# A residual block with a SwiGLU: finer steps beside the plain blocks, rms without a reciprocal, the last three down blocks by halves of the tokens

## Chip, cores and metric

The kernel runs on 1 core of one Trainium2 chip. The metric is the device time of one execution in microseconds (us), as the median of several runs. TensorE (PE in the rows) does the matmuls, VectorE (DVE) and ScalarE (ACT) prepare operands and take results out of PSUM, GpSimd (POOL) does four small products at the end, and SyncE (SP) issues the DMAs. Each engine runs its own queue in order and waits on semaphores of the others.

## What is computed

One layer of a streaming encoder on 512 tokens of width 1024, all float32: two gated token mixers, cross attention to 256 memory tokens, a SwiGLU of width 2816 and a final norm. The change touches only the SwiGLU and the norms around it:

```python
def _rms(t, w):
    tf = t.astype(jnp.float32)
    y = tf * lax.rsqrt(jnp.mean(tf * tf, axis=-1, keepdims=True) + EPS)
    return y.astype(t.dtype) * w

def _swiglu(h, w_gate, w_up, w_down):
    return (jax.nn.silu(h @ w_gate) * (h @ w_up)) @ w_down

def reference(...):
    ...
    x = x + _swiglu(_rms(x, norm_ffn_w[l]), w_ffn_gate[l], w_ffn_up[l], w_ffn_down[l])
    return _rms(x, norm_final_w)
```

## The kernel before

**Arithmetic and layout.** Activations lie transposed: `res[0]` to `res[7]` are the residual stream, 128 features by 512 tokens each. Each float32 operand is split into a high part (ScalarE, a cast) and a low part (VectorE, the difference), and a product is three matmuls: high by high, high by low, low by high. `unit()` loads a weight tile R (`wp`, three buffers), and makes H (ScalarE, L100) and L (VectorE, L101) of it. A load into R waits until the last reader of the tile three before it is done.

**The SwiGLU's plain part.** Hidden blocks 0 to 4 are computed plainly: ten blocks of 24 matmuls of 512 columns, `outs[0]` to `outs[9]`, a gate and an up block in turn, from the unnormalised stream. They go to four PSUM buffers `ps_mm`, so that block 4 writes where block 0 was and needs that `plain_act(0)` has read it. `plain_act(j)` multiplies the gate by the norm's factor `n2.b` (VectorE, L1178), takes the silu (ScalarE), multiplies by the up block (L1180) and splits the product into `act[j]`. The table `beside` (L1192 to 1203) says for each block what VectorE and ScalarE do beside it, and both follow the order in which the code is written (`manual_schedule`):

- `squares` and `norm_2`: the sums of squares of the stream. ScalarE squares into one buffer `sq`, VectorE adds. TensorE sums over the features, VectorE computes rsqrt (`rt_n`) in 9 small operations, TensorE transposes and spreads it (`t<-ident,rt_n`), ScalarE copies it to `n2.b` (`rb_n`, L234).
- `sums(i)` and `splits(i)`: combinations of the stream's token halves (`zx`, 10 VectorE operations for one i) and their split into `z_t1` to `z_t4`, operands of the next part.
- `scale_stream`: `rms` is the reciprocal of `n2.b` (VectorE, L1073), and the stream is multiplied by it (L1075, 8 operations), so that later sums need no other factor. What follows adds to the stream scaled so.
- `weight_side(5)`: loads R of group 5, and sums of its quarters (SA, SB), each split into SH and SL, and DH and DL.

**The groups.** Hidden blocks 5 to 21 are computed by a scheme with seven products in place of eight, `group(j)`: products r11, r21, t2, t1, t3, r22, t4 (L1125), each 12 matmuls of 256 columns. Product t2 writes the PSUM buffer of r11 and so waits for ScalarE's copy of it (`t2k<-mm`, L1140). Between products stand down blocks (`down`), which add the part of the output that is ready to the stream; in the first group the first of them follows t3. Here TensorE follows the code; the order on VectorE and ScalarE is set by a scheduler.

**The last part.** Eight last down blocks, j = 0 to 7, of 15 matmuls each, 512 columns, the last one in two halves of 256 tokens. Behind each, VectorE adds to the stream (L1249), ScalarE squares and multiplies by the final weight (L1252). After a half of block 7 comes `n3`: sums on TensorE (`t<-ones`), rsqrt on VectorE, transposes (`t<-ident,rt_n`) to the one PSUM buffer `ps_t`, the final products `fin` (L1261, L1267 on VectorE, L1265 on GpSimd) that read it, and four output DMAs.

Of the kernel before, what the change touches and what calls it, by code (L numbers as in the profile page):

```python
# [16 lines left out]
ALU = mybir.AluOpType  # L17
# [19 lines left out]
def build(tc, a, out):  # L37
# [46 lines left out]
    def f(ap):  # L84
        return ap.bitcast(F32)
# [97 lines left out]
    class Norm:  # L183
# [850 lines left out]
    def act_tile(n):  # L1034
        return fp.tile([P, 2, S], F32R, tag="a", bufs=9, name=uniq(n))
# [11 lines left out]
    def sums(i):
        tiles = [act_tile("zx") for _ in range(3)]
        x12, x1, x2, x3, x4 = [f(x)[:, e].rearrange("p (k c) -> p k c", k=2) for x in tiles for e in range(2)][:5]
        for e in range(2):  # L1050
            k, q = 2 * i + e, 4 + 2 * i + e
            wa, wb = wf_w[:, k : k + 1], wf_w[:, q : q + 1]

            def stt(o, x, w, y, op):
                nc.vector.scalar_tensor_tensor(out=o[:, e], in0=x, scalar=w, in1=y[:, e], op0=ALU.mult, op1=op)  # L1055

            nc.vector.tensor_scalar_mul(x12[:, e], res[k][:, t1], wa)
            stt(x1, res[k][:, t0], wa, x12, ALU.subtract)
            stt(x2, res[q][:, t1], wb, x1, ALU.add)
            stt(x3, res[q][:, t1], wb, x12, ALU.subtract)  # L1060
            stt(x4, res[q][:, t0], wb, x2, ALU.subtract)
        token_sums[i] = x1, x2, x3, x4

    def splits(i):
        x1, x2, x3, x4 = token_sums[i]
        for o, x, sign in (("t2", x2, -1.0), ("t1", x1, -1.0), ("t3", x3, None), ("t4", x4, -1.0)):
            split(zt[o][:, 2 * i : 2 * i + 2, 0], zt[o][:, 2 * i : 2 * i + 2, 1], x, sign)
# [23 lines left out]
    def weight_side(j):  # L1091

        q0, q1 = slice(0, 512), slice(512, 1024)
        w = a["w_fgu"][j - NPLAIN]
        r0 = wp.tile([P, 1024], F32, tag="R", bufs=3, name=uniq("R"))
        r1 = wp.tile([P, 1024], F32, tag="R", bufs=3, name=uniq("R"))
        sa = fw.tile([P, 2, 512], F32, tag="S", bufs=2, name=uniq("SA"))
        sb = fw.tile([P, 2, 512], F32, tag="S", bufs=2, name=uniq("SB"))  # L1100
# [92 lines left out]
    first_weights = []  # L1193
    beside = {
        0: [lambda: squares(range(4))],
        1: [lambda: squares(range(4, 8)), norm_2],
        2: [lambda: sums(0), lambda: plain_act(0)],
        3: [lambda: splits(0)],
        4: [lambda: plain_act(1), lambda: sums(1)],
        5: [lambda: splits(1)],  # L1200
        6: [lambda: plain_act(2), lambda: scale_stream(range(2))],
        7: [lambda: scale_stream(range(2, KC))],
        8: [lambda: plain_act(3), lambda: first_weights.append(weight_side(NPLAIN))],
        9: [],
    }
    plain = [a[n][j] for j in range(NPLAIN) for n in ("w_fg", "w_fu")]
    us = [unit(x) for x in plain[:2]]
    outs = []
    with tc.manual_schedule(engines={mybir.EngineType.DVE, mybir.EngineType.Activation}):
# [31 lines left out]
    for j in range(KC):
        units = down_units(len(PARTS) - 1, j)

        W = S if j < KC - 1 else S // 2
        for c0 in range(0, S, W):
            cs = slice(c0, c0 + W)
            pb = ps_mm()
            down_block(pb[:, :W], len(PARTS) - 1, units, cs)
            nc.vector.tensor_tensor(out=res[j][:, cs], in0=res[j][:, cs], in1=pb[:, :W], op=ALU.add)  # L1249
            n3.add(res[j][:, cs], cols=cs, last=j == KC - 1)  # L1250
            if j < KC - 1:
                nc.scalar.activation(res[j], res[j], AF.Copy, scale=wo_w[:, j : j + 1])  # L1252
                continue
            n3.finish(cols=cs, eps=eps)
            for i in (7, 6, 0, 1, 2, 3, 4, 5):
                if i % 2 == (1 if i > 5 else 0):
                    fin = xwp.tile([P, S], F32R, tag="xw", bufs=16, name=uniq("fin"))
                    f3 = f(fin).rearrange("p (e c) -> p e c", e=2)
                o = f3[:, i % 2]
                if i == j:  # L1260
                    nc.vector.scalar_tensor_tensor(  # L1261
                        out=o, in0=res[i][:, cs], scalar=wo_w[:, i : i + 1], in1=n3.ps, op0=ALU.mult, op1=ALU.mult
                    )
                elif i in (3, 5):
                    nc.gpsimd.tensor_tensor(out=o, in0=res[i][:, cs], in1=n3.b, op=ALU.mult)  # L1265
                else:
                    nc.vector.tensor_tensor(out=o, in0=res[i][:, cs], in1=n3.ps, op=ALU.mult)  # L1267
                if i % 2 == (0 if i > 5 else 1):
                    nc.sync.dma_start(out[i // 2][:, :, cs], f3)
# [80 lines left out]
```

## Time and profile before

| | |
|---|---|
| median of 3 runs | 926.15 us (925.33 to 926.57) |
| the profiled execution | 926.71 us |
| its span | 924.9 us |
| TensorE busy | 892.9 us, 97% |
| VectorE busy | 674.4 us, 73% |
| ScalarE busy | 476.6 us, 52% |

The span runs from the first to the last instruction on record; the execution is 1.8 us longer. The share of TensorE is so high that only two kinds of place are of interest: those at which it waits, and those at which its matmuls are longer than elsewhere. A list of what each engine waited for, a timeline of each engine, and the granted clock in short windows show both.

### The profile page before, as it was taken

Reading aid. Unit: us, or ns where it says so; the run is one execution under the profiler, and the core shown is the slowest. Engines: PE = TensorE matmul, PEld = TensorE weight load, DVE = VectorE, ACT = ScalarE, POOL = GpSimd, SP = SyncE. Lnnn points to the kernel's source line nnn. Section 1 sums busy time; section 2 is a strip of 40 time slices with the busy share of each in tenths; the row PEclk is TensorE's granted clock in tenths of the full one; section 3 lists DMA queues with packets and bytes.
Section 4 is the critical chain, followed back from the end, with each engine's and each line's share of the span. In section 5 each row is a group of like instructions: output and inputs, shape, how many; then the busy total and the mean of one; then the engine's idle time right before and its main releaser. Section 6 shows DMA issues by size and latency. Waiting matters only on the chain.

```text
span 924.9 us, 12952 instructions
## 1 busy us (share of the span) xinstructions
PE 892.9 (97%) x4879; PEld 761.5 (82%) x4879; DVE 674.4 (73%) x1338; ACT 476.6 (52%) x869; POOL 7.1 (1%) x31
## 2 busy tenths in 40 slices
PE   8999999999999999999999998979999999999994
PEld 6898888887888787778888786869999989899983
DVE  6777888787344959957767986887777786788654
ACT  7576674657334748463435854343444444444451
POOL 1000000000000000000000000000000000000001
PEclk9999999999999999999999998989999999999996
DMA  7332222222332131425332131233232332332312
GB/s 243 95 114 69 69 69 69 69 69 69 97 109 69 48 102 58 135 69 172 101 130 99 47 98 62 82 99 110 86 103 93 103 112 93 103 120 68 91 44 91
DMA packets 31726, 86.20 MB, mean 93 GB/s; under 512 B 4304, under 2 KB 8016, under 8 KB 31664
## 3 DMA queue, kind: packets, MB, share of 16 engines
q1 hardware_dynamic: 31520, 85.37, 29.4%
q8 instruction: 38, 0.62, 0.3%
q14 instruction: 24, 0.20, 0.1%
q10 hardware_dynamic: 144, 0.00, 0.0%
HBM read 83.27 MB, written 2.10 MB: 92 GB/s over the span
## 4 chain that ended last, share of the span: by engine, by line
PE 70%; DVE 15%; DMA 7%; ACT 5%; issue 2%; SPq 0%; DVEq 0%; ACTq 0%
PE mm L82 52%; PE mm L1125 7%; DMA R<-in_w_fd 4%; PE s L1125 3%; PE s L82 3%; PE o L82 3%; DVE L L101 2%; DMA R<-in_w_fgu 2%; DVE SL L101 2%; ACT H L100 1%; PE t L82 1%; PE t L551 1%; DVE zx L1055 1%; DMA R<-in_w_tg 1%; ACT pm L96 1%
## 5 line engine op out<-in xcount | busy, mean ns | idle before, releaser
L100 ACT CAST H<-R 128x1024 fp32r<-128x1024 f32 (+4 forms) x137 | 123.8, 905 | 175.8 <-PE mm L82 120.4
L101 DVE TENSOR_TENSOR L<-R,H 128x1024 fp32r<-128x1024 f32 (+4 forms) x137 | 142.5, 1042 | 53.1 <-ACT H L100 52.5
L82 PE MATMUL mm<-xh,H 128*128 128x512 f32 x320 | 125.7, 394 | 3.9 <-DVE t2k L1178 3.9
L82 PE MATMUL mm<-xl,H 128*128 128x512 f32 x320 | 127.4, 398 | 0.0
L82 PE MATMUL mm<-xh,L 128*128 128x512 f32 x320 | 127.2, 398 | 0.0
L82 PE MATMUL mm<-a,H 128*128 128x512 f32 (+1 forms) x362 | 110.2, 386 | 0.0
L82 PEld LDWEIGHTS mm<-a,H 128*128 128x128 f32 x362 | 65.3, 188 | 11.4
L82 PEld LDWEIGHTS mm<-xh,H 128*128 128x128 f32 x320 | 60.9, 190 | 16.6 <-issue 4.3
L82 PE MATMUL mm<-H,xh 128*128 128x512 f32 (+1 forms) x192 | 70.5, 367 | 0.0
L82 PEld LDWEIGHTS mm<-xl,H 128*128 128x128 f32 x320 | 60.8, 190 | 11.7
L82 PE MATMUL mm<-L,xh 128*128 128x512 f32 (+1 forms) x192 | 70.3, 366 | 0.0
L82 PE MATMUL mm<-H,xl 128*128 128x512 f32 (+1 forms) x192 | 70.1, 365 | 0.0
L82 PEld LDWEIGHTS mm<-xh,L 128*128 128x128 f32 x320 | 60.8, 190 | 11.1
L82 PE MATMUL mm<-a,L 128*128 128x512 f32 (+1 forms) x181 | 69.3, 383 | 0.0
L1125 PE MATMUL mm<-z_t,SH 128*128 128x256 f32 x272 | 50.2, 284 | 3.1 <-ACT t2k L1140 2.7
L96 ACT ACTIVATE p<-sm,nm,sc 128x256 f32<-128x256 f32 (+1 forms) x64 | 36.3, 569 | 25.3 <-DVE es L525 20.3
L1125 PEld LDWEIGHTS mm<-z_t,SH 128*128 128x128 f32 x272 | 42.7, 191 | 5.0 <-ACT t2k L1140 3.3
L82 PEld LDWEIGHTS mm<-L,xh 128*128 128x128 f32 x192 | 36.1, 188 | 5.4 <-DVE L L101 0.6
L82 PEld LDWEIGHTS mm<-H,xh 128*128 128x128 f32 x192 | 36.3, 189 | 5.2 <-ACT H L100 0.2
L1125 PE MATMUL mm<-xh,SH 128*128 128x256 f32 x136 | 38.6, 284 | 1.9 <-ACT SH L100 1.9
L82 PEld LDWEIGHTS mm<-H,xl 128*128 128x128 f32 x192 | 36.1, 188 | 5.1
L82 PEld LDWEIGHTS mm<-a,L 128*128 128x128 f32 x181 | 34.0, 188 | 7.0
(354 smaller groups left out, 2095.8 us busy)
## 6 DMA issues: line engine op xcount, KB each, us to landing
R<-in_w_fgu SPq DMA_DIRECT2D x34, 512.0 KB, 4.0
R<-in_w_gate SPq DMA_DIRECT2D x16, 512.0 KB, 3.5
R<-in_w_fd SPq DMA_DIRECT2D x24, 256.0 KB, 2.6
R<-in_w_fd SPq DMA_DIRECT2D x16, 320.0 KB, 2.9
x<-in_xT SPq DMA_DIRECT2D x16, 256.0 KB, 3.3
R<-in_w_q SPq DMA_DIRECT2D x8, 512.0 KB, 3.9
R<-in_w_attn_o SPq DMA_DIRECT2D x8, 512.0 KB, 3.5
R<-in_w_vg SPq DMA_DIRECT2D x8, 512.0 KB, 3.5
```

The source lines that it names most:

```text
L82: nc.tensor.matmul(o, lhsT=lhsT, rhs=rhs, start=start, stop=stop)
L96: last_table[0] = nc.scalar.activation(*args, **kw)
L100: nc.scalar.copy(out=hi, in_=src)
L101: nc.vector.tensor_tensor(out=lo, in0=src, in1=f(hi), op=ALU.subtract)
L551: nc.tensor.transpose(out=pt[:, i * P : (i + 1) * P], in_=prs[i // 2][:, i % 2, b * P : (b + 1) * P], identity=ident)
L1055: nc.vector.scalar_tensor_tensor(out=o[:, e], in0=x, scalar=w, in1=y[:, e], op0=ALU.mult, op1=op)
L1125: nc.tensor.matmul(o, lhsT=l_, rhs=r_, start=first and k == 0 and i == 0, stop=k == 3 and i == 2, skip_group_check=not first,)
```

## The change

It has four pieces.

1. **Steps beside the plain blocks.** `squares` use a tile each pair, not one `sq`. `sums(i)` is called in halves, and its first operation (x12, a multiplication by a weight) goes from VectorE to ScalarE. `norm_2` moves from block 1 to block 2, and `plain_act` becomes a generator whose three steps are placed one by one.
2. **rms.** In place of the reciprocal, `v * rsqrt(v)` is formed on 128x4 values (one VectorE operation), transposed and spread by four more matmuls into the PSUM buffer `o`, and copied by ScalarE to `rms`.
3. **weight_side(5)** is a generator too, started in block 7, and the first down block's weights are loaded in block 9's place (`first_units`) and not when the down block is reached.
4. **The last part.** Blocks 5, 6 and 7 are all done by halves: first tokens 0 to 255 of the three, then tokens 256 to 511.

```diff
-            sq = acc
-            if not first:
+            if first:
+                sq = acc
+            elif sq is None:
                 sq = tp.tile([P, S], F32, tag="sq", bufs=1, name=uniq("sq"))[:, :w]
...
-            nc.vector.tensor_scalar_mul(x12[:, e], res[k][:, t1], wa)
+        nc.scalar.activation(x12[:, e], res[k][:, t1], AF.Copy, scale=wa)
...
-        if js[0] == 0:
-            nc.vector.reciprocal(rms, n2.b)
...
     def norm_2():
         n2.finish()
+        rt = alr[:, 0, NT : 2 * NT]
         nc.vector.tensor_scalar_mul(eps, n2.v, EPS)
+        nc.vector.tensor_tensor(out=rt, in0=n2.v, in1=n2.tok, op=ALU.mult)
+        pb = ps_o()
+        for t in range(NT):
+            mm(pb[:, t * P : (t + 1) * P], rt[:, t : t + 1].broadcast_to([P, P]), ident, True, True)
+        return pb
...
-        2: [lambda: sums(0), lambda: plain_act(0)],
...
+        [lambda: pb.append(norm_2()), lambda: sums(0, 1), lambda: next(acts[0]), lambda: splits(0, ("t2", "t1"))],
...
+        [lambda: scale_stream((4, 5, 6, 7)), lambda: first_units.append(down_units(0, 0))],
...
+    steps = [(j, slice(0, S)) for j in range(KC - 3)]
+    for cs in (t0, t1):
+        steps += [(j, cs) for j in range(KC - 3, KC)]
+    for j, cs in steps:
```

**VectorE behind the second norm.** `rt_n` is the rsqrt, `zx` are the sums of the first pair of features, L1178 (after: L1184) is the first operation of `plain_act(0)`, which block 4 needs. Before:

```order
L181 SCALAR_TENSOR_TENSOR rt_n_1057_5532<-nwt_5534,nwy_5533 128x4
L1189 TENSOR_SCALAR alr<-v_n_1056_5530 128x4
L101 TENSOR_TENSOR L_5553<-R_5551,H_5552 128x1024
L1057 TENSOR_SCALAR zx_5582<-x_0_4470,wf_w 128x256
L1055 SCALAR_TENSOR_TENSOR zx_5582<-x_0_4470,wf_w,zx_5582 128x256
L1055 SCALAR_TENSOR_TENSOR zx_5583<-x_4_4632,wf_w,zx_5582 128x256 x2
L1055 SCALAR_TENSOR_TENSOR zx_5584<-x_4_4632,wf_w,zx_5583 128x256
L1057 TENSOR_SCALAR zx_5582<-x_1_4509,wf_w 128x256
L1055 SCALAR_TENSOR_TENSOR zx_5582<-x_1_4509,wf_w,zx_5582 128x256
L1055 SCALAR_TENSOR_TENSOR zx_5583<-x_5_4673,wf_w,zx_5582 128x256 x2
L1055 SCALAR_TENSOR_TENSOR zx_5584<-x_5_4673,wf_w,zx_5583 128x256
L1178 TENSOR_TENSOR t2k_5595<-mm_5447,rb_n_1061_5548 128x512
```

After:

```order
L181 SCALAR_TENSOR_TENSOR rt_n_1061_5568<-nwt_5570,nwy_5569 128x4
L1204 TENSOR_SCALAR alr<-v_n_1060_5566 128x4
L1205 TENSOR_TENSOR alr<-v_n_1060_5566,rt_n_1061_5568 128x4
L1058 SCALAR_TENSOR_TENSOR zx_5522<-x_1_4509,wf_w,zx_5522 128x256
L1058 SCALAR_TENSOR_TENSOR zx_5523<-x_5_4673,wf_w,zx_5522 128x256 x2
L1058 SCALAR_TENSOR_TENSOR zx_5524<-x_5_4673,wf_w,zx_5523 128x256
L1184 TENSOR_TENSOR t2k_5598<-mm_5447,rb_n_1065_5584 128x512
```

The weight tile's L and the sums' first half now stand ahead of the norm, and both x12 are on ScalarE, so that four operations of `zx` lie between the norm and the first step of `plain_act(0)` and not ten and an L.

**ScalarE at the first group.** H and R are the weights of the down blocks (640 columns) and R of 1024 columns that of group 6; SH and DH belong to the weight sides; the last row is the copy for which product t2 waits. Before:

```order
L100 CAST SH_5847<-R_5841 128x1024
L100 CAST H_6028<-R_6027 128x640
L100 CAST SH_5855<-SB_5844 128x1024
L100 CAST SH_5859<-SA_5843 128x1024
L100 CAST DH_5863<-R_5842 128x512
L100 CAST SH_6056<-R_6050 128x1024
L1140 COPY t2k_5904<-mm_5902 128x256
```

After:

```order
L100 CAST SH_5850<-SB_5811 128x1024
L1189 CAST a_5855<-t2k_5845 128x512
L100 CAST SH_5857<-SA_5810 128x1024
L100 CAST DH_5861<-R_5809 128x512
L100 CAST H_5896<-R_5895 128x640
L100 CAST H_6031<-R_6030 128x640
L100 CAST SH_6059<-R_6053 128x1024
L1143 COPY t2k_5913<-mm_5911 128x256
```

The weight side of group 5 is done earlier against the plain blocks, and the casts of the two down weights stand behind it; the copy stands behind group 6's first cast in both. On SP the load of that R (R_6053) stands behind all loads up to the second down weight, and it goes to the buffer whose last reader is the DL of group 5.

**VectorE at the end.** `fin` are the final products of the first half of the tokens; L1249 (after: L1279) adds a down block to the stream; `acc_n` gathers squares; L223 (after: L224) begins the second half's norm. Before:

```order
L1261 SCALAR_TENSOR_TENSOR fin_8953<-x_7_4755,wo_w,t_8948 128x256
L1267 TENSOR_TENSOR fin_8953<-x_6_4714,t_8948 128x256
L1267 TENSOR_TENSOR fin_8957<-x_0_4470,t_8948 128x256
L1267 TENSOR_TENSOR fin_8957<-x_1_4509,t_8948 128x256
L1267 TENSOR_TENSOR fin_8961<-x_2_4550,t_8948 128x256
L1267 TENSOR_TENSOR fin_8965<-x_4_4632,t_8948 128x256
L223 SCALAR_TENSOR_TENSOR v_n_1591_8993<-t_8988,alr 128x2
```

After:

```order
L1291 SCALAR_TENSOR_TENSOR fin_8956<-x_7_4755,wo_w,t_8951 128x256
L1297 TENSOR_TENSOR fin_8956<-x_6_4714,t_8951 128x256
L1297 TENSOR_TENSOR fin_8960<-x_0_4470,t_8951 128x256
L1297 TENSOR_TENSOR fin_8960<-x_1_4509,t_8951 128x256
L1297 TENSOR_TENSOR fin_8964<-x_2_4550,t_8951 128x256
L1297 TENSOR_TENSOR fin_8968<-x_4_4632,t_8951 128x256
L1279 TENSOR_TENSOR x_6_4714<-x_6_4714,mm_8993 128x256
L1279 TENSOR_TENSOR x_7_4755<-x_7_4755,mm_9014 128x256
L209 TENSOR_TENSOR acc_n_8720<-acc_n_8720,sq_9010 128x256
L224 SCALAR_TENSOR_TENSOR v_n_1593_9038<-t_9033,alr 128x2
```

The first half's final products now stand ahead of the last two additions, and on TensorE the transposes that they need stand 19 matmuls of 256 columns ahead of the last one, where before they stood behind it.

## Rows read from the trace of the kernel before

**Rows 1.** Page, busy time, share of the span and instructions of each engine.

```profile
PE 892.9 (97%) x4879; PEld 761.5 (82%) x4879; DVE 674.4 (73%) x1338; ACT 476.6 (52%) x869; POOL 7.1 (1%) x31
```

**Rows 2.** TensorE's waits from 550 us on: total us, times, longest us.

```profile
PE mm L82 <- DVE t2k L1178: 3.9, 1, 3.9
...
PE t L82 <- DVE fin L1267: 2.7, 1, 2.7
PE mm L1125 <- ACT t2k L1140: 2.7, 1, 2.7
```

**Rows 3.** Window: its length, busy time by engine, PEclk, DMA share, GB/s.

```profile
570.00:575.00 5.00, 5.00 (x12) 3.94 (x13) 3.64 (x5) 4.25 (x8) 0.00 (x0) 0.50 0.03 8
```

**Rows 4.** TensorE at blocks 3 and 4: start, duration, line, operation, operands.

```profile
565.39 0.39 PE L82 MATMUL mm<-xl,H 128*128 128x512 f32 x1
565.62 0.39 PE L82 MATMUL mm<-xh,L 128*128 128x512 f32 x1
...
575.13 0.40 PE L82 MATMUL mm<-xh,H 128*128 128x512 f32 x1
```

**Rows 5.** TensorE, the last plain matmul, product t2, and down block 0.

```profile
604.86 0.39 PE L82 MATMUL mm<-xh,L 128*128 128x512 f32 x1
...
615.52 0.51 PE L1125 MATMUL mm<-z_t,SH 128*128 128x256 f32 x2 [2.68 <-ACT t2k L1140]
...
621.80 0.63 PE L82 MATMUL mm<-a,H 128*128 128x512 f32 x2
```

**Rows 6.** ScalarE: the copy of norm 2, group 6's cast, product t2's copy.

```profile
562.14 0.59 ACT L234 COPY rb_n<-t 128x512 f32<-128x512 f32 x1 [4.99 <-PE t L82]
...
614.15 1.04 ACT L100 CAST SH<-R 128x1024 fp32r<-128x1024 f32 x1
615.11 0.37 ACT L1140 COPY t2k<-mm 128x256 f32<-128x256 f32 x1
```

**Rows 7.** VectorE from norm 2 to the end of group 5's weight side.

```profile
560.67 0.16 DVE L181 SCALAR_TENSOR_TENSOR rt_n<-nwt,nwy 128x4 f32<-128x4 f32 x1
...
563.71 1.23 DVE L101 TENSOR_TENSOR L<-R,H 128x1024 fp32r<-128x1024 f32 x1 [2.80 <-ACT H L100]
564.85 0.35 DVE L1057 TENSOR_SCALAR zx<-x,wf_w 128x256 f32<-128x256 f32 x1
565.24 1.80 DVE L1055 SCALAR_TENSOR_TENSOR zx<-x,wf_w,zx 128x256 f32<-128x256 f32 x4
...
570.42 0.69 DVE L1180 TENSOR_TENSOR t2k<-t2k,mm 128x512 f32<-128x512 f32 x1 [0.70 <-ACT t2k L96]
...
593.02 3.35 DVE L1073 RECIPROCAL rms<-rb_n 128x512 f32<-128x512 f32 x1
...
598.75 3.69 DVE L1075 TENSOR_TENSOR x<-x,rms 128x512 f32<-128x512 f32 x6
...
609.52 0.82 DVE L101 TENSOR_TENSOR L<-R,H 128x640 fp32r<-128x640 f32 x1
...
615.06 0.69 DVE L101 TENSOR_TENSOR DL<-R,DH 128x512 fp32r<-128x512 f32 x1
```

**Rows 8.** Window from the end of `rt_n` to the end of DL, VectorE's busy time alone.

```profile
560.83:615.75 54.92, 44.24 (x68) 0.91 0.25 79
```

**Rows 9.** DMA issues from 590 to 625 us: count, KB each, median us to landing.

```profile
R<-in_w_fgu SPq DMA_DIRECT2D x4, 512.0 KB, 3.8
```

**Rows 10.** TensorE in the last down block, and the norms of its two halves.

```profile
903.00 0.40 PE L82 MATMUL mm<-a,H 128*128 128x256 f32 x2
...
904.79 0.40 PE L82 MATMUL mm<-a,H 128*128 128x256 f32 x2
...
909.32 0.88 PE L82 MATMUL t<-ident,rt_n 128*128 128x128 f32 x4 [1.46 <-DVE rt_n L181]
912.93 0.56 PE L82 MATMUL t<-ones,acc_n 128*128 128x2 f32 x2 [2.72 <-DVE fin L1267]
...
916.69 1.19 PE L82 MATMUL t<-ident,rt_n 128*128 128x128 f32 x4 [1.92 <-DVE rt_n L181]
```

More of the change, by code (lines that the diff above doesn't have):

```diff
@@ L1045, in build, with sums, stt, splits @@
     token_sums = {}
[L1047 to L1055, printed above, removed]
-            nc.vector.tensor_scalar_mul(x12[:, e], res[k][:, t1], wa)
[L1058 to L1065, printed above, removed]
+    def sums(i, e):
+        if e == 0:
+            tiles = [act_tile("zx") for _ in range(3)]
+            xs = [f(x)[:, h].rearrange("p (k c) -> p k c", k=2) for x in tiles for h in range(2)]
+            token_sums[i] = xs[:5]
+        x12, x1, x2, x3, x4 = token_sums[i]
+        k, q = 2 * i + e, 4 + 2 * i + e
+        wa, wb = wf_w[:, k : k + 1], wf_w[:, q : q + 1]
+        def stt(o, x, w, y, op):
+            nc.vector.scalar_tensor_tensor(out=o[:, e], in0=x, scalar=w, in1=y[:, e], op0=ALU.mult, op1=op)
+        nc.scalar.activation(x12[:, e], res[k][:, t1], AF.Copy, scale=wa)
+        stt(x1, res[k][:, t0], wa, x12, ALU.subtract)
+        stt(x2, res[q][:, t1], wb, x1, ALU.add)
+        stt(x3, res[q][:, t1], wb, x12, ALU.subtract)
+        stt(x4, res[q][:, t0], wb, x2, ALU.subtract)
+    def splits(i, which):
+        _, x1, x2, x3, x4 = token_sums[i]
         for o, x, sign in (("t2", x2, -1.0), ("t1", x1, -1.0), ("t3", x3, None), ("t4", x4, -1.0)):
-            split(zt[o][:, 2 * i : 2 * i + 2, 0], zt[o][:, 2 * i : 2 * i + 2, 1], x, sign)
+            if o in which:
+                split(zt[o][:, 2 * i : 2 * i + 2, 0], zt[o][:, 2 * i : 2 * i + 2, 1], x, sign)
     rms = cp.tile([P, S], F32, tag="rb", bufs=2, name="rms")
     def scale_stream(js):
-        if js[0] == 0:
-            nc.vector.reciprocal(rms, n2.b)
         for i in js:
@@ L1179, in plain_act @@
         table_act(t, t, AF.Silu)
+        yield
         nc.vector.tensor_tensor(out=t, in0=t, in1=outs[2 * j + 1], op=ALU.mult)
-        hidden(j, t)
+        act[j] = act_tile("a")
+        nc.scalar.copy(out=act[j][:, 0], in_=t)
+        yield
+        nc.vector.tensor_tensor(out=act[j][:, 1], in0=t, in1=f(act[j][:, 0]), op=ALU.subtract)
+        yield
     def squares(js):
         for i in js:
-            n2.add(res[i])
+            if i % 2 == 1:
+                sqs.append(f(act_tile("sq")))
+            n2.add(res[i], sq=sqs[-1][:, i % 2] if sqs else None)
     def norm_2():
         n2.finish()
+        rt = alr[:, 0, NT : 2 * NT]
         nc.vector.tensor_scalar_mul(eps, n2.v, EPS)
-    eps = alr[:, 0, 0:NT]
[L1193 to L1196, printed above, removed]
-        2: [lambda: sums(0), lambda: plain_act(0)],
[L1198 to L1205, printed above, removed]
+        nc.vector.tensor_tensor(out=rt, in0=n2.v, in1=n2.tok, op=ALU.mult)
[3 more added lines that the diff above has]
+        return pb
+    sqs, first_weights = [], []
+    eps = alr[:, 0, 0:NT]
     plain = [a[n][j] for j in range(NPLAIN) for n in ("w_fg", "w_fu")]
@@ L1208, in build @@
     outs = []
+    pb = []
+    acts = [plain_act(j) for j in range(NPLAIN)]
+    ws = weight_side(NPLAIN)
+    beside = [
+        [lambda: squares(range(4))],
+        [lambda: squares(range(4, 8)), lambda: sums(0, 0)],
+        [lambda: pb.append(norm_2()), lambda: sums(0, 1), lambda: next(acts[0]), lambda: splits(0, ("t2", "t1"))],
+        [lambda: next(acts[0]), lambda: splits(0, ("t3", "t4")), lambda: next(acts[0])],
+        [lambda: next(acts[1]), lambda: sums(1, 0), lambda: next(acts[1]), lambda: sums(1, 1), lambda: next(acts[1])],
+        [lambda: nc.scalar.copy(out=rms, in_=pb[0]), lambda: splits(1, ("t2", "t1", "t3", "t4"))],
+        [lambda: next(acts[2]), lambda: scale_stream((0, 1)), lambda: next(acts[2]), lambda: scale_stream((2, 3)),
+         lambda: next(acts[2])],
+        [lambda: next(ws)],
+        [lambda: next(acts[3]), lambda: next(ws), lambda: next(acts[3]), lambda: first_weights.append(next(ws)),
+         lambda: next(acts[3])],
+        [lambda: scale_stream((4, 5, 6, 7)), lambda: first_units.append(down_units(0, 0))],
+    ]
     with tc.manual_schedule(engines={mybir.EngineType.DVE, mybir.EngineType.Activation}):
@@ L1216, in build @@
                 do()
-        plain_act(NPLAIN - 1)
+        for _ in acts[NPLAIN - 1]:
+            pass
     with tc.manual_schedule(engines={mybir.EngineType.PE}):
@@ L1240, in build @@
     n3 = Norm("n3", S)
[L1241 to L1269, printed above, removed]
@@ new lines, in build @@
+    last = len(PARTS) - 1
+    halved = {}
+    steps = [(j, slice(0, S)) for j in range(KC - 3)]
+    for cs in (t0, t1):
+        steps += [(j, cs) for j in range(KC - 3, KC)]
+    for j, cs in steps:
+        W = cs.stop - cs.start
+        if j not in halved:
+            halved[j] = down_units(last, j)
+        pb = ps_mm()
+        down_block(pb[:, :W], last, halved[j], cs)
+        nc.vector.tensor_tensor(out=res[j][:, cs], in0=res[j][:, cs], in1=pb[:, :W], op=ALU.add)
+        n3.add(res[j][:, cs], cols=cs, last=j == KC - 1)
+        if j < KC - 1:
+            nc.scalar.activation(res[j][:, cs], res[j][:, cs], AF.Copy, scale=wo_w[:, j : j + 1])
+            continue
+        n3.finish(cols=cs, eps=eps)
+        for i in (7, 6, 0, 1, 2, 3, 4, 5):
+            if i % 2 == (1 if i > 5 else 0):
+                fin = xwp.tile([P, S], F32R, tag="xw", bufs=16, name=uniq("fin"))
+                f3 = f(fin).rearrange("p (e c) -> p e c", e=2)
+            o = f3[:, i % 2]
+            if i == j:
+                nc.vector.scalar_tensor_tensor(
+                    out=o, in0=res[i][:, cs], scalar=wo_w[:, i : i + 1], in1=n3.ps, op0=ALU.mult, op1=ALU.mult
+                )
+            elif i in (3, 5):
+                nc.gpsimd.tensor_tensor(out=o, in0=res[i][:, cs], in1=n3.b, op=ALU.mult)
+            else:
+                nc.vector.tensor_tensor(out=o, in0=res[i][:, cs], in1=n3.ps, op=ALU.mult)
+            if i % 2 == (0 if i > 5 else 1):
+                nc.sync.dma_start(out[i // 2][:, :, cs], f3)
```

11 lines of the change are left out of this document (7 added, 4 removed).

## The prediction, as it was put on record

> **What bounds the kernel now.** I read the page's busy times first: TensorE is busy 892.9 of 924.9 us [rows 1]. So nothing that VectorE or ScalarE save counts by itself; it counts where TensorE waits for them. Second, the list of TensorE's waits: the three largest behind the plain blocks' start are at block 4 (3.9 us, for the first step of `plain_act(0)`), at the final norm's second half (2.7 us, for the first half's final products) and at product t2 of the first group (2.7 us, for ScalarE's copy) [rows 2]. Third, the granted clock. After the wait at block 4 it is at 0.50, the 1.2 GHz level, and only 12 matmuls pass in 5 us [rows 3]. So each long wait has a second price behind it. Both together are read as distances between starts:
>
> - Block 4: the last matmul before the wait starts at 565.62, one takes 0.23, and the twelve slow ones end where the next starts, at 575.13 [rows 4]. Thirteen steps of 0.23 would be 2.95 us, they took 9.51: 6.56 us are lost.
> - First group: from the end of the plain part (604.86 + 0.23 = 605.09) to the first down block (621.80) pass 16.7 us [rows 5], for five products of 12 matmuls of 256 columns. At 0.119 each (1.79 us for 15, [rows 10]) that is 7.2: 9.5 us are lost.
> - End: the last down block's matmuls end at 909.32 − 1.46 = 907.86, and the second norm's transposes start at 916.69 [rows 10]. What follows (final products, output DMAs) is the same after the change.
>
> Between the first group and the last part the order of all engines is the same before and after, and the list of waits names none there that comes near these three, so a gain made up to 621.80 is carried to the last part whole.
>
> **The change, part by part.** *Plain part.* The norm's sums stand one matmul later (0.23) and four transposes are added. Four such took 0.88 at the end [rows 10]; I take 0.95, between 0.5 (if they slip in behind others) and 1.2. Is the wait at block 4 gone? `rt_n` ends at 560.83 [rows 7], after the change at 561.06. From there to the copy's end pass 562.14 + 0.59 − 560.83 = 1.9 us [rows 6], then x12 on ScalarE (not shown; between 0.37 for a copy of 256 columns and 0.59 for one of 512, [rows 6]; I take 0.42), four operations of `zx` in 1.80 and the step itself, 0.69 [rows 7]: 565.9. Block 4 can start at 565.85 + 0.23 + 0.95 = 567.0. So the wait goes, by 1.1 us. Plain end: 605.09 − 6.56 + 0.95 = 599.5 (the norm's sums are moved, not added).
>
> *First group.* r11 and r21 find their weights ready, since the weight side now starts in block 7: 24 × 0.113 to 0.119, until about 602.3. Then TensorE needs the copy, and the order on ScalarE puts it behind group 6's cast, which needs group 6's R, whose load waits for DL. In the rows of before, too, the copy came straight after that cast (614.15, then 615.11) [rows 6], while TensorE was in its wait of 2.68 us [rows 5].
>
> So the time of DL decides, not the end of the plain part. From the end of `rt_n` to the end of DL, VectorE was busy 44.24 of 54.92 us, idle 10.7 [rows 8]. Of the busy time go, by [rows 7]: the reciprocal 3.35; four of the six multiplications by rms (4 × 0.615 = 2.46) and two L of 640 columns (2 × 0.82), which now stand behind DL; four x12 (1.40); four `zx` (1.80) and one L (1.23), now ahead of the norm; one split of an act (0.69), now behind DL. The 128x4 product adds 0.16. 44.24 − 12.57 + 0.16 = 31.8. The idle time I take as 9.4: eight places where the order makes VectorE wait for one or two ScalarE operations, at 0.7 (as at L1180, [rows 7]) to 1.7 each. Three of the eight are the x12, each of which VectorE now takes from ScalarE. Bounds: 5.6 (all eight at 0.70) and 10.7 (as before). DL then ends at 561.06 + 31.8 + 9.4 = 602.3 (598.5 to 603.6), and before at 615.75.
>
> From there: load 3.8 [rows 9], cast 0.96 to the next start, copy 0.41 to the start of t2 (615.52 − 615.11) [rows 5, 6]: t2 starts at 607.5. TensorE will have waited 5.2 us, longer than the 2.68 before, so I take the stretch behind it as it was, slow matmuls included: 621.80 − 615.52 = 6.28 [rows 5]. Down block 0 starts at 613.8 in place of 621.80: **8.0 us gained** (6.7 to 11.8). The 6.56 of block 4 is no separate term: it moves the wait to t2, where VectorE's chain ends.
>
> A rule speaks against the x12 move. On VectorE one took 0.35 [rows 7]; on ScalarE it costs VectorE a wait where it isn't covered, 0.70 at L1180 [rows 7]. The Trainium skill, "ScalarE: Activation LUTs", "Rules for kernel authors", gives multiplications to VectorE and not to ScalarE. By the rule the move lengthens the chain by three times 0.35; if instead the x12 were wholly covered, three waits of 0.70 would fall out of the idle time, DL would come 2.1 sooner, and the gain here would be 10.1. I go with the bare wait; no row of before shows this operation on ScalarE.
>
> *rms.* The reciprocal is in the sum above. ScalarE's copy of `rms` (0.59) lies beside blocks; if ScalarE were late there, the multiplications would wait, and with them DL, one for one; that is within the bounds of the idle time.
>
> *Last part.* Two more blocks by halves: a pair of halves is 2 × 1.79 = 3.58 against 15 × 0.227 = 3.40 [rows 4, 10], so +0.4 us. The first half's sums and transposes now stand between matmuls: 0.88 for the transposes more ahead of the last matmul, and some 0.3 for a wait on `rt_n`. Last matmul: 907.86 + 1.6 = 909.4. The first half's transposes start some 3.2 us ahead of that, at 906.2, and copy and final products took 912.93 − 909.32 = 3.6 from there [rows 10], so VectorE has them behind it at 909.8. Then follow one another an addition, and on ScalarE a square, a multiplication and a square, 0.37 to 0.42 each by the copy of 256 columns [rows 6]: 911.5. The second norm's sums are complete from there, and don't begin at 912.93 behind the final products [rows 10]: 1.4 us sooner. One of its four pairs of sums doesn't need the last square (0.4 to 0.56 sooner, [rows 10]), and at the full clock all are shorter. I take **2.1 us** (0 to 2.8).
>
> Sum: 8.0 + 2.1 = 10.1. The profiled execution took 926.71, so 916.6; it lies 0.56 above the median of the runs shown, so a median of 916.0 to 916.6. I say 916.3.
>
> **The rivals.**
>
> *No wait at t2.* If VectorE idles under 4 us up to DL, t2 starts at once: down block 0 at 599.5 + 7.2 = 606.7, 15.1 gained, with the end 17.2: 909.5. For it: no reciprocal, fewer handoffs in a row. Against: eight known waits at 0.70 are already 5.6.
>
> *The wait at block 4 stays.* The margin is 1.1 us. Then the plain part ends at about 606, r21 at 609, and the copy of 607.5 is there: no wait at t2, down block 0 at some 613.5. It costs almost nothing: 916 to 917.
>
> *The end gives nothing,* if the first half's final products keep VectorE until the second half is late by as much as it now is: 926.7 − 8.0 = 918.7. For it: they now stand ahead of the last two additions on VectorE. Against: only 1.7 us of other work follows them up to the sums.
>
> *Slower: the handoffs.* From `rt_n` to DL I count 29 VectorE operations that read a ScalarE result. The new order alternates the two engines more finely. If each handoff cost 0.70 us bare, none covered, VectorE would idle 20.3 us and DL end at 613.2: t2 at 618.4, down block 0 at 624.7, 2.9 later than before, and the end's 2.1 doesn't pay for it: 927.5. It decides at 0.67 us per handoff (19.5 us idle); at 1 us it would be 936. Against it: about as many in the old order left 10.7 us idle in all [rows 8].
>
> *In between,* VectorE idle 13 to 19 us: 920 to 926.
>
> **How the numbers follow.** Forecast 0.62; block 4 still waits 0.07; the end gives nothing 0.12; no wait at t2 0.05; in between 0.08; slower 0.06. The range reaches from 912 (idle time at its lower bound, with the end's best) to 921 (the end gives nothing and the idle time is 1 us over its upper bound); it leaves out no wait, slower and most of in between, 0.17. About 0.2%, 1.85 us, is what a measurement here can tell from no change. Faster by more than that: 0.91 (all but slower and a part of in between); within it 0.04; slower 0.05.
>
> **What would show it.** In the profile after: TensorE without a wait at block 4 and no clock of 0.50 there; L1184 ending about a microsecond ahead of block 4; a wait of 4 to 7 us at t2 for the copy L1143, that copy right behind group 6's cast, that cast behind a load issued when DL ends near 602; a slow stretch behind it; down block 0 near 614; at the end the sums of the second half near 903 to 904, that is some 2 us sooner after the shift of 8 is taken off. If DL comes before 598 or after 606, or the copy comes ahead of the cast, the sum is wrong there; if L1151's waits in the groups grow, the gain was not carried.

## The result, and the profile after

| | before | after |
|---|---|---|
| median | 925.74 us (924.15 to 926.57) | 914.59 us (912.96 to 915.40) |
| ratio | | 0.9879, 95% interval 0.9859 to 0.9899 |
| profiled execution | 926.71 us | 915.01 us |
| its span | 924.9 us | 913.2 us |

The change makes the kernel 11.2 us faster; the forecast was 916.3, some 10 us. The busy times, on the page of the kernel after (busy time, share, instructions of each engine):

```profile
PE 888.4 (97%) x4917; PEld 760.6 (83%) x4917; DVE 670.3 (73%) x1338; ACT 479.3 (52%) x878; POOL 7.0 (1%) x31
```

Against [rows 1], VectorE has lost 4.1 us, ScalarE has gained 2.7, and TensorE is busy 4.5 us less although it has 38 matmuls more; part of that is the low clock behind block 4, which is gone (windows below). TensorE's waits from 545 us on, the four largest of the kernel after (total, times, longest):

```profile
PE mm L1128 <- ACT t2k L1143: 6.0, 2, 5.7
PE t L82 <- DVE rt_n L181: 1.9, 1, 1.9
PE s L1128 <- DVE s L1154: 1.7, 4, 0.7
PE t L82 <- DVE acc_n L209: 1.7, 1, 1.7
```

Of [rows 2] the wait of block 4 and that for `fin` are gone, and the one for ScalarE's copy at t2 has grown from 2.7 to 5.7 us. The three places of the prediction, one after another:

TensorE behind block 4 and behind the wait at t2, in windows of the kernel after (length, busy by engine, granted clock, DMA share, GB/s):

```profile
570.00:575.00 5.00, 5.00 (x24) 4.14 (x23) 3.63 (x5) 2.78 (x5) 0.00 (x0) 1.00 0.37 112
...
605.00:610.00 5.00, 2.63 (x12) 2.63 (x13) 4.81 (x8) 2.46 (x4) 0.00 (x0) 0.50 0.53 179
610.00:615.00 5.00, 5.00 (x33) 4.74 (x33) 4.06 (x7) 2.38 (x4) 0.00 (x0) 0.85 0.27 76
```

The window that passed 12 matmuls at 0.50 [rows 3] now passes 24 at 1.00. Behind t2 a slow stretch remains: the clock is at 0.50 from 605 to 610.

TensorE's rows of the kernel after, at the end of the plain part, product t2 and down block 0 (start, duration, operation, and in brackets the idle time ahead and who ended it):

```profile
598.45 0.39 PE L82 MATMUL mm<-xh,L 128*128 128x512 f32 x1
...
607.37 0.80 PE L1128 MATMUL mm<-z_t,SH 128*128 128x256 f32 x2 [5.71 <-ACT t2k L1143]
...
613.52 0.63 PE L82 MATMUL mm<-a,H 128*128 128x512 f32 x2
```

What t2 waits for, link by link: VectorE's DL, SyncE's issue of group 6's load, ScalarE's cast of it and the copy behind (kernel after):

```profile
601.51 0.68 DVE L101 TENSOR_TENSOR DL<-R,DH 128x512 fp32r<-128x512 f32 x1
```

```profile
602.22 0.33 SPq L1102 DMA_DIRECT2D R<-in_w_fgu  x1
```

```profile
606.00 1.04 ACT L100 CAST SH<-R 128x1024 fp32r<-128x1024 f32 x1 [3.90 <-DMA R<-in_w_fgu]
606.96 0.37 ACT L1143 COPY t2k<-mm 128x256 f32<-128x256 f32 x1
```

Each row begins where the one above ends: DL ends at 602.19, the load is issued at 602.22, ScalarE is idle 3.90 us until it has landed, casts, copies, and t2 starts. In the kernel before, DL did not hold t2: group 6's load was issued 5.4 us ahead of DL's end, and t2 started 0.2 us ahead of it (615.52 against 615.75 [rows 5, 7]).

```profile
610.37 0.33 SPq L1101 DMA_DIRECT2D R<-in_w_fgu  x1
```

So DL ends 13.6 us sooner after the change, and t2 starts only 8.15 us sooner: the 5.2 us of load, cast and copy now come behind DL.

The end, TensorE in the kernel after: the first half's transposes and the matmul behind them, the last down matmul, the second half's sums and transposes:

```profile
896.65 0.68 PE L82 MATMUL t<-ident,rt_n 128*128 128x128 f32 x4
897.09 0.36 PE L82 MATMUL mm<-a,L 128*128 128x256 f32 x1
...
899.32 0.28 PE L82 MATMUL mm<-a,L 128*128 128x256 f32 x1
901.29 0.35 PE L82 MATMUL t<-ones,acc_n 128*128 128x2 f32 x2 [1.70 <-DVE acc_n L209]
901.65 0.59 PE L82 MATMUL t<-ones,sq 128*128 128x2 f32 x2
...
905.01 1.19 PE L82 MATMUL t<-ident,rt_n 128*128 128x128 f32 x4 [1.92 <-DVE rt_n L181]
```

The first half's transposes stand between matmuls, and the second half's sums come 1.7 us behind the last matmul; before they came 5.1 behind it [rows 10].

Between these places, the last addition to the stream in the groups (VectorE), before and then after:

```profile
879.40 0.69 DVE L1174 TENSOR_TENSOR x<-x,mm 128x512 f32<-128x512 f32 x1
```

```profile
870.30 0.69 DVE L1179 TENSOR_TENSOR x<-x,mm 128x512 f32<-128x512 f32 x1
```

So the 11.7 us of the two spans divide as follows: 621.80 − 613.52 = 8.3 up to down block 0; (879.40 − 621.80) − (870.30 − 613.52) = 0.8 in the groups; (924.9 − 879.40) − (913.2 − 870.30) = 2.6 in the last part.

### The profile page after: what moved, and what is told of

The parts are those of the page before. It is cut to its first block, busy times and chain, and to the rows that moved or that the text cites. A ratio compares the mean times of both kernels' runs of the same rounds, so it can differ in the third digit from the quotient of the medians.

```text
span 913.2 us, 13045 instructions
## 1 busy us (share of the span) xinstructions
PE 888.4 (97%) x4917; PEld 760.6 (83%) x4917; DVE 670.3 (73%) x1338; ACT 479.3 (52%) x878; POOL 7.0 (1%) x31
## 4 chain that ended last, share of the span: by engine, by line
PE 78%; DVE 11%; DMA 4%; ACT 4%; issue 2%; SPq 0%; DVEq 0%; ACTq 0%
PE mm L82 55%; PE mm L1128 10%; PE s L1128 4%; PE s L82 3%; PE o L82 3%; DMA R<-in_w_fd 2%; DVE L L101 2%; DMA R<-in_w_fgu 1%; DVE SL L101 1%; PE t L82 1%; DMA x<-in_xT 1%; ACT H L100 1%; PE t L552 1%; ACT SH L100 1%; ACT pm L96 1%
## 5 line engine op out<-in xcount | busy, mean ns | idle before, releaser
L82 PEld LDWEIGHTS mm<-a,H 128*128 128x128 f32 x382 | 67.6, 189 | 10.6
L82 PE MATMUL mm<-a,L 128*128 128x512 f32 (+1 forms) x191 | 71.2, 373 | 0.0
L82 PEld LDWEIGHTS mm<-a,L 128*128 128x128 f32 x191 | 36.0, 188 | 6.5
L101 DVE TENSOR_TENSOR SL<-SB,SH 128x1024 fp32r<-128x1024 f32 x17 | 20.8, 1226 | 24.8 <-ACT SH L100 24.8
```

What stands on the lines that cost most here:

```text
L82: nc.tensor.matmul(o, lhsT=lhsT, rhs=rhs, start=start, stop=stop)
L101: nc.vector.tensor_tensor(out=lo, in0=src, in1=f(hi), op=ALU.subtract)
```

## Experiments

**Theory:** two independent gains. The larger one is set by VectorE's chain from the second norm to DL, by way of group 6's load, cast and copy; the wait at block 4 costs nothing of its own as long as t2 waits longer. The smaller one is the last part. **Rivals:** the gain at the front is the wait at block 4 itself; it comes from the finer steps and not from the reciprocal; the last part's gain is only a shift. All ratios are to the kernel before on the same chip. `c0_after` is the kernel after once more. e1, e3 and e4 ran beside it, e2, e5, e6 and e7 later on the same chip, e9 and e10 on another.

> The changed kernel once more, beside the experiments on the same chip: 914 to 915 us, 11 below the kernel before. In its profile the wait at product t2 for the copy L1143 is 5.5 to 6 us, block 4 doesn't wait, and the first down block starts near 613.5.

Measured: 915.27 us, ratio 0.9874 (0.9855 to 0.9893), t2 at 606.66 behind a wait of 5.69 us, last addition in the groups at 870.81.

**The last part taken back** (`e1_tail_whole`), and **the last part alone, on the kernel before** (`e2_tail_halves`: the same loop the other way round):

```diff
-    steps = [(j, slice(0, S)) for j in range(KC - 3)]
-    for cs in (t0, t1):
-        steps += [(j, cs) for j in range(KC - 3, KC)]
-    for j, cs in steps:
...
+    for j in range(KC):
...
+        W = S if j < KC - 1 else S // 2
+        for c0 in range(0, S, W):
```

> The changed kernel, but the last part as before (down blocks 0 to 6 whole, block 7 in halves). If the last part gave its own gain (the second half's sums no longer behind the first half's final products), 2.1 us (as predicted) to 2.6 us (as the two traces differ there) are lost: 917. Rival, that the shift seen there is only the groups' and the plain part's gain carried on: no change, 914.6. All up to the last part is as in the changed kernel.

> The kernel before with the new last part alone (down blocks 5 to 7 by halves). The change with the old last part lost 3.1 us, so if the last part's gain stands by itself it is 2.5 to 3.1 us here too: 923 to 924 against 926 to 927 of before. Rival, that it needs what comes ahead: no change.

Measured: e1 918.39, 0.9913 (0.9898 to 0.9927), 3.1 us over c0. e2 923.33, 0.9962 (0.9950 to 0.9975), 3.2 under the kernel before. TensorE's row of the second half's sums in e1, and then in e2:

```profile
904.05 0.56 PE L82 MATMUL t<-ones,acc_n 128*128 128x2 f32 x2 [2.72 <-DVE fin L1293]
```

```profile
910.75 0.35 PE L82 MATMUL t<-ones,acc_n 128*128 128x2 f32 x2 [1.70 <-DVE acc_n L208]
```

The wait for `fin` comes and goes with the loop, whatever happens ahead. The piece is worth 3.1 to 3.2 us and adds to the rest; that it gives nothing is excluded. What is left of the change, e1 against the kernel before, is 926.84 − 918.39 = 8.4 us.

**The reciprocal put back** (`e3_reciprocal`), in the place where ScalarE's copy of `rms` now stands:

```diff
-        [lambda: nc.scalar.copy(out=rms, in_=pb[0]), lambda: splits(1, ("t2", "t1", "t3", "t4"))],
+        [lambda: nc.vector.reciprocal(rms, n2.b), lambda: splits(1, ("t2", "t1", "t3", "t4"))],
```

> The changed kernel, but rms is again the reciprocal on VectorE (3.35 us), in the place where the copy from PSUM stood, without the four transposes and the 128x4 product. If VectorE's chain from the norm to DL sets the start of product t2, DL and with it the whole rest come 3.2 us later, the wait at t2 grows to about 9 us (the plain part ends 0.95 sooner) and the time is 917.8. Rival, that TensorE's plain part sets it and the wait at t2 has slack: 0.95 faster, 913.6.

Measured: 920.14, 0.9927 (0.9915 to 0.9940), 4.9 over c0 and 2.3 over what was expected. VectorE and TensorE in e3:

```profile
582.73 3.35 DVE L1220 RECIPROCAL rms<-rb_n 128x512 f32<-128x512 f32 x1
...
604.89 0.68 DVE L101 TENSOR_TENSOR DL<-R,DH 128x512 fp32r<-128x512 f32 x1
```

```profile
590.31 0.47 PE L82 MATMUL mm<-xh,H 128*128 128x512 f32 x1 [2.12 <-DVE t2k L1184]
...
610.81 0.79 PE L1128 MATMUL mm<-z_t,SH 128*128 128x256 f32 x2 [6.55 <-ACT t2k L1143]
```

From the end of `rt_n` to the end of DL pass 45.0 us (560.55 to 605.57) where c0 has 41.8 (559.68 to 601.51): 3.2 longer for 3.35 us of work, nearly one for one. The remaining 0.9 by which DL and t2 are late against c0 lies ahead of `rt_n`, where the two kernels are the same. The new wait of 2.12 at a plain block doesn't count: t2 waits behind it all the same, even longer. The last addition in the groups is at 876.38, 5.6 later than in c0, t2 is 4.15 later, so another 1.4 us was lost behind down block 0; the waits for VectorE's `s` there sum to 3.3 us where c0 has 1.6. That the finer steps alone made the gain falls: of the 8.4 us at the front, 4.9 go when the reciprocal comes back. Some 3.5 us are left for the finer steps and the earlier weight side together; no run takes these two apart.

**The wait at block 4 put back** (`e4_act_late`): the three steps of `plain_act(0)` stand behind all splits of the first sums.

```diff
-        [lambda: pb.append(norm_2()), lambda: sums(0, 1), lambda: next(acts[0]), lambda: splits(0, ("t2", "t1"))],
-        [lambda: next(acts[0]), lambda: splits(0, ("t3", "t4")), lambda: next(acts[0])],
+        [lambda: pb.append(norm_2()), lambda: sums(0, 1), lambda: splits(0, ("t2", "t1"))],
+        [lambda: splits(0, ("t3", "t4")), lambda: next(acts[0]), lambda: next(acts[0]), lambda: next(acts[0])],
```

> The changed kernel, but the three steps of plain_act(0) stand behind all splits of the first sums, so that block 4 waits again, about 3.4 us by the trace, with slow matmuls behind it; the work on VectorE up to DL is the same in sum. If VectorE's chain to DL decides, the plain part ends near 604.5, r21 near 607, the copy at about 607 is there, the wait at t2 and the slow stretch behind it are gone: the first down block starts between 611.5 and 613.5 and the time is 912.6 to 914.6. Rival, that the wait at block 4 is a term of its own: 3.4 + 2.4 = 5.8 us slower, 920.4.

Measured: 913.07, 0.9852 (0.9835 to 0.9868), 2.2 us under c0. TensorE in e4, at block 4 and at t2:

```profile
568.69 0.47 PE L82 MATMUL mm<-xh,H 128*128 128x512 f32 x1 [2.85 <-DVE t2k L1184]
...
606.39 0.50 PE L1128 MATMUL mm<-z_t,SH 128*128 128x256 f32 x2 [1.96 <-ACT t2k L1143]
```

The rival, 5.8 us slower, falls clearly: with a wait of 2.85 us at block 4 the kernel isn't slower. That it is faster isn't shown, since the intervals of e4 and c0 overlap. The plain part ends 3.5 us later than in c0, and t2, which waits for another engine, starts 0.3 sooner: what TensorE waits ahead of it is taken off the wait at t2 (5.69 to 1.96). From the end of `rt_n` to the end of DL pass 41.1 us in e4 and 41.8 in c0: between 562 and 572 us VectorE waits 1.22 and 1.21 us for the splits in c0, and 0.70, 0.69 and 0.26 in their place in e4, 0.8 us less. Down block 0 starts at 612.23; in three executions with the long wait at t2 it started at 612.91 (e1), 613.52 (kernel after) and 613.76 (c0).

**x12 back on VectorE** (`e6_x12_vector`), all four, of which three stand behind the norm: the place at which a rule had spoken against the change:

```diff
-        nc.scalar.activation(x12[:, e], res[k][:, t1], AF.Copy, scale=wa)
+        nc.vector.tensor_scalar_mul(x12[:, e], res[k][:, t1], wa)
```

> The changed kernel with x12 (the first operation of each half of the sums) on VectorE again. The trace shows three waits of VectorE for x12 behind the norm, 2.1, 1.1 and 1.1 us; an x12 there costs 0.35. If these waits fall away and nothing takes their place, DL and t2 come 2 to 3.3 us sooner: 911 to 912.6. Rival, that the next ScalarE result (the silu, the splits) is late instead: no change, 914.6, or 1 us slower for the three operations added.

Measured: 910.74, 0.9825 (0.9809 to 0.9841), 4.5 us under c0. In the kernel after, ScalarE takes 0.51 for an x12, and VectorE is idle ahead of each `zx` that needs one:

```profile
562.16 0.51 ACT L1060 ACTIVATE zx<-x,wf_w 128x256 f32<-128x256 f32 x1
```

```profile
562.71 1.80 DVE L1058 SCALAR_TENSOR_TENSOR zx<-x,wf_w,zx 128x256 f32<-128x256 f32 x4 [2.14 <-ACT zx L1060]
...
575.55 1.80 DVE L1058 SCALAR_TENSOR_TENSOR zx<-x,wf_w,zx 128x256 f32<-128x256 f32 x4 [1.10 <-ACT zx L1060]
...
579.10 1.80 DVE L1058 SCALAR_TENSOR_TENSOR zx<-x,wf_w,zx 128x256 f32<-128x256 f32 x4 [1.15 <-ACT zx L1060]
```

The second of them in ScalarE's queue, kernel after: the x12 stands behind the silu, which waits for VectorE.

```profile
574.49 0.63 ACT L96 ACTIVATE t2k<-t2k 128x512 f32<-128x512 f32 x1 [2.22 <-DVE t2k L1184]
575.02 0.49 ACT L1060 ACTIVATE zx<-x,wf_w 128x256 f32<-128x256 f32 x1
```

So VectorE hands over L1184, ScalarE does the silu and then the x12, and VectorE waits for both. In e6 VectorE does one itself in 0.35, and TensorE waits less at t2:

```profile
560.87 0.35 DVE L1060 TENSOR_SCALAR zx<-x,wf_w 128x256 f32<-128x256 f32 x1
```

```profile
604.61 0.80 PE L1128 MATMUL mm<-z_t,SH 128*128 128x256 f32 x2 [2.55 <-ACT t2k L1143]
```

Three waits of 2.14, 1.10 and 1.15 us stand against three operations of 0.35: 4.39 − 1.05 = 3.3 us. From the end of `rt_n` to the end of DL the chain went from 41.8 to 38.6, by 3.2. The median gained more, 4.5; by the last addition in the groups (867.02) the profiled execution is 3.3 us ahead of the kernel after and 3.8 ahead of c0. From t2 to down block 0 pass 5.6 us in e6, but 5.7 to 7.1 in the three executions named under e4, so what a shorter wait at t2 spares behind it isn't shown. The move to ScalarE was a loss inside a change that gains. The Trainium skill, "ScalarE: Activation LUTs", "Rules for kernel authors", gives multiplications to VectorE. The runs agree, 4.5 us in the median, though the 3.3 us lie in what VectorE waits for and not in the 0.16 us by which ScalarE's operation is longer.

**The copy ahead of the cast** (`e5_copy_first`): group 6's first cast may only be issued behind r11's copy, so that the copy doesn't stand behind a cast that waits for a DMA.

```diff
-        h0, l0 = pair_of(r0)
+        if j == NPLAIN + 1:
+            with tc.issue_after(copies[0].ins):
+                h0, l0 = pair_of(r0)
+        else:
+            h0, l0 = pair_of(r0)
```

> The changed kernel with one edge more: on ScalarE group 6's first cast follows the copy of r11, not the other way. If only ScalarE's order holds product t2, t2 starts at about 601.7 in place of 607, without a slow stretch, the first down block at about 606 (its L ends at 605.9), and 5 to 7.5 us are gained: 907 to 910. Rival, that VectorE's chain is the bound in any case and the groups behind give it back in waits for group 6's SL and s: under 2 us, 913 to 914.6.

**Both, e5's and e6's edits** (`e7_both`):

> The copy ahead of the cast and x12 on VectorE together. If the copy's place on ScalarE is the only hold of t2, the second edit adds nothing to the first, since t2 already starts right behind r21: 907 to 910, as with the copy alone. If VectorE's chain still holds the groups behind, it adds up to 3 us: 905 to 907.

Measured: e5 912.24, 0.9845 (0.9831 to 0.9859), 3.0 under c0 and short of the 907 to 910 expected; e7 910.08, 0.9822 (0.9805 to 0.9840). TensorE in e5 at t2 and at the next product that waits for such a copy, and the ScalarE rows ahead of the latter:

```profile
602.34 0.50 PE L1132 MATMUL mm<-z_t,SH 128*128 128x256 f32 x2 [0.71 <-ACT t2k L1147]
...
607.78 0.50 PE L1132 MATMUL mm<-z_t,SH 128*128 128x256 f32 x2 [2.34 <-ACT t2k L1154]
```

```profile
605.89 1.04 ACT L100 CAST SH<-R 128x1024 fp32r<-128x1024 f32 x1 [3.60 <-DMA R<-in_w_fgu]
606.84 0.62 ACT L96 ACTIVATE t2k<-t2k 128x512 f32<-128x512 f32 x1
607.37 0.35 ACT L1154 COPY t2k<-mm 128x256 f32<-128x256 f32 x1
```

t2 starts 4.3 us sooner than in c0, so it was the copy's place in ScalarE's queue that held it. But the cast still waits for its load, and now the next copy stands behind it: of the 4.3 us the median keeps 3.0. In e7 t2 follows r21 without a wait, down block 0 starts at 605.70, 7.8 us sooner than in the kernel after, and yet e7 can't be told from e6. TensorE of e7 at t2 and further on, and ScalarE:

```profile
601.04 0.40 PE L1132 MATMUL mm<-z_t,SH 128*128 128x256 f32 x2
...
626.59 0.51 PE L1132 MATMUL mm<-z_t,SH 128*128 128x256 f32 x2 [1.80 <-ACT t2k L1154]
```

```profile
625.54 0.72 ACT L100 CAST H<-R 128x640 fp32r<-128x640 f32 x1 [3.54 <-DMA R<-in_w_fd]
626.17 0.37 ACT L1154 COPY t2k<-mm 128x256 f32<-128x256 f32 x1
```

The same pattern, a copy behind a cast that waits 3.54 us for its load, now in the middle of the groups. From down block 0 to the last addition pass 259.7 us in e7 and 256.8 in the kernel after.

**The remaining order of the chain** (`e9_scale_behind`: e6, and the first four multiplications by rms moved behind DL; `e10_late_x12`: e4's and e6's edits together):

```diff
-        [lambda: next(acts[2]), lambda: scale_stream((0, 1)), lambda: next(acts[2]), lambda: scale_stream((2, 3)),
-         lambda: next(acts[2])],
+        [lambda: next(acts[2]), lambda: next(acts[2]), lambda: next(acts[2])],
...
-        [lambda: scale_stream((4, 5, 6, 7)), lambda: first_units.append(down_units(0, 0))],
+        [lambda: scale_stream(range(8)), lambda: first_units.append(down_units(0, 0))],
```

> x12 on VectorE, and all eight multiplications by rms behind DL (four of them stood ahead of it). If each VectorE operation ahead of DL counted in full, DL and t2 would come 2.46 us sooner than with x12 on VectorE alone: 908.3. By the theory only what is not covered counts: two of the four pairs filled VectorE's waits for the silu and the cast of plain_act(2), 0.70 each, which come back bare, so about 1.1 us sooner, 909.6 (not told apart from 910.7 by the time alone, but by DL and t2 in the trace).

> x12 on VectorE, and the three steps of plain_act(0) behind the first splits. If an early wait of TensorE that costs no clock is free as long as VectorE's chain sets t2, block 4 waits 1 to 2 us, the wait at t2 (2.55 with x12 on VectorE alone) goes and with it the slow stretch: first down block 1.5 to 2 us sooner, 908.7 to 909.3. Rival, that the two waits add: 1 to 2 us slower than with x12 alone, 912.

Measured: e9 910.89, 0.9839 (0.9826 to 0.9853); e10 910.37, 0.9825 (0.9810 to 0.9841); both lie over what was expected (909.6, and 908.7 to 909.3). In e9 the chain from `rt_n` to DL is 38.1 us against 38.6 in e6, half a microsecond for 2.5 us of work moved away: VectorE waited for other things instead. In e10 down block 0 starts at 609.21, 1.0 sooner than in e6, and the last addition in the groups is at 867.04 (867.02 in e6): given back. Neither is told apart from e6. e6, e7, e9 and e10 all lie between 910.1 and 910.9 and beat both kernels; e6 does it with one line.

## Why the prediction was right, step by step

| | before | forecast | after | off by |
|---|---|---|---|---|
| end of `rt_n` | 560.83 | 561.06 | 560.36 | 0.7 early |
| end of the plain part | 605.09 | 599.5 | 598.68 | 0.8 early |
| end of DL | 615.75 | 602.3 | 602.19 | 0.1 early |
| start of t2 | 615.52 | 607.5 | 607.37 | 0.1 early |
| down block 0 | 621.80 | 613.8 | 613.52 | 0.3 early |

- **The wait at block 4 goes, and is no term of the sum.** Both right. TensorE doesn't wait there, and e4 shows that the wait put back costs nothing. `rt_n` ended 0.7 earlier than reckoned; c0 and e4 run the same code up to there and have 559.68 and 560.00, so that step moves by some tenths between executions.
- **DL decides.** Right: e5, which takes the copy out from behind the cast, starts t2 4.3 us sooner than c0, though DL ends 0.6 later. The size is right too: busy 31.95 of 41.83 us in the kernel after, so idle 9.88, where 31.8 and 9.4 were reckoned. VectorE's window from the end of `rt_n` to the end of DL (length, then busy of PE, PEld, DVE, ACT and POOL):

```profile
560.36:602.19 41.83, 41.31 (x201) 34.63 (x200) 31.95 (x52) 22.21 (x33) 0.00 (x0) 1.00 0.21 67
```

- **The idle time's parts were wrong and cancelled,** so that their sum came out within 0.5 us is luck. The three x12 were reckoned at 0.70 us of waiting each, 2.1 together; they took 4.39. The other places, reckoned at 7.3, took 5.5. The row at L1180 [rows 7] was too kind a neighbour: there ScalarE did one operation, while the x12 stand in ScalarE's queue behind another one that itself waits for TensorE (the copy `rb_n`) or for VectorE (the rows of e6's section). And x12 itself took 0.51, not 0.42. The prediction found no row of before with this operation on ScalarE, but there is one in the last part, for 512 columns (L1252, a multiplication by a weight), beside squares, which have no scale from memory:

```profile
903.92 0.63 ACT L202 ACTIVATE sq<-x 128x512 f32<-128x512 f32 x1 [2.01 <-DVE x L1249]
904.59 0.72 ACT L1252 ACTIVATE x<-x,wo_w 128x512 f32<-128x512 f32 x1
905.64 0.42 ACT L202 ACTIVATE sq<-x 128x256 f32<-128x256 f32 x1 [0.33 <-DVE x L1249]
```

A square of 256 columns and the 0.09 us more with the scale are the 0.51 measured. The rule set against the move had the direction right and the size too small: 1.05 us on the chain by the prediction, 3.2 in e6.
- **From DL to down block 0.** Load, cast, copy: 607.37 − 602.19 = 5.2, as reckoned. The stretch behind t2 took 6.15, reckoned 6.28 as before [rows 5], with the low clock again (0.50). That they agree so well is luck in part: behind the same wait it took 7.10 in c0 and 5.69 in e1.
- **The reciprocal.** Its 3.35 us lie on the chain nearly one for one (e3: 3.2). The median lost more, 4.9; whether the reciprocal also causes the 0.9 us ahead of `rt_n` and the 1.4 behind down block 0 isn't shown.
- **The groups carry the gain.** Nearly: 0.8 us were added there, and in other runs some was taken (against the kernel after, e3 lost 1.7 there, e7 2.9, e10 1.0). The time from down block 0 to the last addition isn't a constant: it lay between 256.3 and 259.7 us. In e7, the longest, copies of ScalarE stand there behind casts that wait for loads.
- **The last part,** reckoned at 2.1, is worth 3.1 to 3.2 (e1, e2). The second half's sums, foretold for 903 to 904, start at 901.29. Two terms were mis-sized. The first half's transposes and a wait on `rt_n` were to delay the last matmul by 0.88 + 0.3; in the rows above, the next matmul starts 0.44 behind the first transpose, and there is no wait. From the last matmul to the sums 2.1 were reckoned, 1.7 measured. The profiled execution of the kernel after shows only 2.6 us because three of its four pairs of sums took 0.57 to 0.59 each where c0 has 0.36 to 0.38.
- **The rivals.** *The end gives nothing*: excluded by e1 and e2. *The wait at block 4 stays*: it didn't; its price was right in that e4, with such a wait, isn't slower. *Slower by handoffs*: VectorE idled 9.88 us in all where 19.5 were needed, so most of the 29 handoffs are covered; of the uncovered ones the three new ones take 4.39, and the longest, 2.14, is one of them. *No wait at t2*: the kernel after has one of 5.71. Only e7 has none, by another way (the copy ahead of the cast): its down block 0 (605.70) and its time (910.08) come near the 606.7 and 909.5 named, but in e5 and e7 the next copies are late.

## To carry to other kernels

A wait that an engine shows is only a price if nothing waits longer behind it: follow the chain to the last of the waits and reckon there, and what is saved ahead of it comes off that wait. An operation moved to an idle engine costs the engine that needs it not the operation's duration but the handoff, here 1.1 to 2.1 us in place of 0.35; an engine that isn't at its limit is no reason to move work to it. On an in-order engine, look at what stands ahead of a short PSUM copy: a cast that waits for a DMA makes TensorE wait for the DMA, and moving one copy ahead uncovers the next.

## What was not expected of the hardware

The low clock behind a wait of TensorE can't be told from the length of the wait alone. At block 4 the kernel before waits 3.87 us, and the window behind it passes 12 matmuls at 0.50 [rows 3]. e2 runs the same code there and waits 3.90 us, and the same window passes 19 matmuls at 0.78. Counted from the end of the wait, 12 matmuls are slow in the kernel before and 7 in e2:

```profile
569.14 0.77 PE L82 MATMUL mm<-xh,H 128*128 128x512 f32 x1 [3.90 <-DVE t2k L1178]
```

```profile
570.00:575.00 5.00, 5.00 (x19) 3.95 (x19) 4.06 (x7) 4.59 (x7) 0.00 (x0) 0.78 0.12 25
```

In e4 the clock stays at 1.00 behind 2.85 us at the same place:

```profile
570.00:575.00 5.00, 5.00 (x24) 4.12 (x23) 3.00 (x4) 2.56 (x4) 0.00 (x0) 1.00 0.24 69
```

And behind a wait of 1.96 us at t2 it is once at 0.78 (e4, the first row) and all through at 1.00 (e9, the two others, whose t2 starts at 602.85):

```profile
605.00:610.00 5.00, 3.61 (x22) 3.61 (x23) 4.73 (x8) 2.91 (x6) 0.00 (x0) 0.78 0.52 172
```

```profile
600.00:605.00 5.00, 3.04 (x26) 2.84 (x25) 5.00 (x10) 1.83 (x3) 0.00 (x0) 1.00 0.15 53
...
605.00:610.00 5.00, 3.77 (x27) 3.31 (x26) 4.06 (x6) 1.72 (x5) 0.00 (x0) 1.00 0.52 164
```

So the second price of a wait isn't fixed, and not every long wait has one: at block 4 it was 6.56 − 3.87 = 2.7 us in the kernel before, 1.7 in e2 reckoned the same way, and next to none in e4. These runs don't show by what rule.
